# Splits, sums and casts beside the gate and up products in another order, and the norms' squares added on POOL behind each residual update

## The chip, the core and the metric

One core of a Trainium2 chip runs the whole program. The metric is the device time of one execution in microseconds (us). In the text PE is TensorE (its matrix product; PEld its weight load), DVE is VectorE, ACT is ScalarE, POOL is GpSimd, and SP is the engine whose queue issues most DMAs.

## The reference, cut to what matters

Two layers over 1024 latent tokens and 256 context tokens, width 1024, everything in float32. The last layer needs no context output.

```python
for l in range(DEPTH):                       # DEPTH = 2
    last = l == DEPTH - 1
    hl = modulate(rms_norm(x, norm1[l]), sh1, sc1)
    ...
    y_l, y_c = token_mixers(hl, hc, ...)     # attention, recurrence, gating unit, w_out
    x = x + g1[:, None] * y_l
    x = x + g2[:, None] * swiglu(modulate(rms_norm(x, norm2[l]), sh2, sc2), w_ffn_in[l], w_ffn_out[l])
    ...                                      # the same for the context, unless last
return rms_norm(x, final_norm)

def rms_norm(x, g):
    y = x * lax.rsqrt(jnp.mean(x * x, axis=-1, keepdims=True) + EPS)
    return y * g

def swiglu(h, w_in, w_out):
    g, u = jnp.split(h @ w_in, 2, axis=-1)   # w_in: 1024 x 2*2816
    return (jax.nn.silu(g) * u) @ w_out
```

## The kernel before, in words

**Precision.** A float32 operand of a product is split: a cast on ACT rounds it to `fp32r` (`wh`, `oh`), a subtraction on DVE keeps the rest (`wl`, `ol`), and three matmuls (high by high, high by rest, rest by high) make up one float32 product. The function `split` issues the cast and the subtraction.

**Gate and up.** The 2816 columns of gate and of up are 22 tiles `f` of 128 columns. For each tile the kernel computes `h @ gate` and `h @ up` for both halves of the 1024 tokens by a scheme of seven products in place of eight (P1 to P7). The left factors are blocks of the gate weights (A11, A12), of the up weights (A21, A22) and of their sums and differences (S1 to S4), the right factors are such combinations of the tokens. One product is 12 matmuls of 512 columns. In the first layer two more products per tile (CG and CU, 256 columns) serve the context. The products go to three PSUM banks `ffA`, `ffB`, `ffC` per tile, and `evacuate` takes the results out on ACT and DVE: copies `e`, sums, the gate's tanh, and the product of gate and up (`th<-th,e`).

**Sums of weights.** `prepare` splits the blocks. For tile `f` POOL computes, behind the split of A12, the four sums and differences S1 to S4 (`s<-wr`, `s<-wr,wr`, `wr<-wr,wr`, `wr<-wr,s`).

**Units.** `ffn_units` cuts the products into units of two whose weight blocks share one pair of tiles (`wh`, `wl`); there are two such pairs, so a unit's split waits until the unit two before it is through PE. In the last layer the seven products of a tile are three units of two and one unit of one (A22, P4). The splits of a unit are issued beside the products of the unit before it: the first block ahead of that unit's first product, the second ahead of its second one, and beside a unit of one both blocks ahead of its only product.

**Folding.** The results of two tiles (f even, f odd) are combined again, on POOL (`o<-th,th`, `th<-th,th`: four per two tiles), split (`oh` on ACT, `ol` on DVE) and written to DRAM (`pair<-oh`, `pair<-ol`) as the right factors of the seven products of the output projection. Generators do this, and `fold_step` moves each on by one step behind every product.

**Norms.** Behind each residual update `x<-op,mod,x` or `x<-fr,g2h,x` on DVE the squares of x are needed for the next norm. In the kernel before, a lane per piece of tokens does this: a lane is a generator that `fill` moves on where a model of the engines' clocks says that ACT and DVE have room. It squares on ACT (`sq<-x`) and adds on DVE (`acc<-acc,sq`). Then a matmul with ones (`ms<-acc,ones`) sums over the 1024 channels, ACT and DVE make the factor `r` of it, and DVE scales with it.

**Order.** Each engine takes its instructions in the order in which the program was written out. That order is fixed when the program is built, by the loops, the lanes and the clock model. In the first layer the gate and up stage also carries the vector work of the conditioning (`ada<-wr,cz,ada` on DVE, its matmuls `adt`), three steps per tile.

Every instruction is recorded with the line of the same helper (L117), so rows are told apart by their tiles.

Of the kernel before, what the change touches and what calls it, by code (L numbers as in the profile page):

```python
# [12 lines left out]
AF = mybir.ActivationFunctionType  # L13
# [109 lines left out]
def hybrid_block_kernel(  # L123
# [546 lines left out]
    written = {}  # L670

    def running_rinv(g, n, box):

        yield lambda: written.get(g, 0) > 0
        acc = temp(name="acc")[:, :n]
        for k in range(KT):
            yield lambda: written.get(g, 0) > k
            yield [x_at(k, g, n)]
            if k == 0:
                act(acc, x_at(k, g, n), AF.Square)  # L680
            else:
                sq = temp(name="sq")[:, :n]
                act(sq, x_at(k, g, n), AF.Square)
                tt(acc, acc, sq, op=OP.add)
        yield from rms_rinv([], n, D, box, acc)

    def running(pieces):

        boxes = {}
        for g, n in pieces:  # L690
            written.pop(g, None)
            boxes[g] = []
            Lane(running_rinv(g, n, boxes[g]), 4)
        return boxes
# [121 lines left out]
    for l in range(DEPTH):  # L816
# [916 lines left out]
        def out_proj(c):  # L1733
# [8 lines left out]
            for m in range(KT):  # L1742
# [12 lines left out]
                for g, n in OUTP[c]:  # L1755
# [11 lines left out]
                    written[g] = m + 1  # L1767
# [138 lines left out]
        def ffn_units():  # L1906
# [10 lines left out]
            if last:  # L1917
                units.append(([(f, "A22") for f in first], [(f, "P4") for f in first], (0, 1)))
            for f in range(NF):
                head = ([(f, "A11"), (f, "A12")], [(f, "P1"), (f, "P2")] + [(f, "CG")] * (not last), (0, 1))  # L1920
                body = [([(f, "S2"), (f, "S1")], [(f, "P6"), (f, "P5")], (0, 1))]
                body += [([(f, "S3"), (f, "S4")], [(f, "P7"), (f, "P3")], (0, 1))]
                if last:
                    tail = [([(f, "A22")], [(f, "P4")], (0, 0))]
                else:
                    tail = [([(f, "A22"), (f, "A21")], [(f, "P4"), (f, "CU")], (0, 1))]
                if f in first:
                    units += tail if not last else []
                elif f < NF - 1 or last:
# [7 lines left out]
        def ffn_in(side):  # L1937
# [7 lines left out]

            def prepare(u, i):
# [10 lines left out]
                if name == "A11":  # L1957
                    mine[f] = dict(zip("gu", (next_raw(False), next_raw(False))))
# [5 lines left out]
                if name == "A12":  # L1964
                    for s in ("s1", "s2"):
                        r[s] = temp(512, name=s).rearrange("p (k m) -> p k m", m=P)
                    if f < EARLY:
                        gp.tensor_tensor(r["s1"], u1, u2, op=OP.add)
                    gp.tensor_tensor(g1, g1, u1, op=OP.subtract)
                    gp.tensor_tensor(r["s2"], u2, g1, op=OP.subtract)  # L1970
                    if f >= EARLY:
                        gp.tensor_tensor(r["s1"], u1, u2, op=OP.add)
                    gp.tensor_tensor(g2, g2, r["s2"], op=OP.subtract)
# [52 lines left out]
            def fold_even(q, b11, b12):  # L2026
                h, t1 = r32("oh"), temp(name="o1")
                sc.copy(h, b11)
                gp.tensor_tensor(t1, b12, b11, op=OP.subtract)
                yield  # L2030
                lo, h1_ = r32("ol"), r32("oh")
                tt(lo, b11, h, op=OP.subtract)
                put(operand(q, "B11"), h, lo)
                sc.copy(h1_, t1)
                yield
                lo = r32("ol")
                tt(lo, t1, h1_, op=OP.subtract)
                put(operand(q, "T1"), h1_, lo)
                evens.add(q)

            def fold_odd(q, b22):
                while q not in evens:
# [544 lines left out]
```

## Time and profile before

| | us |
|---|---|
| median of 3 runs (lowest to highest) | 3146.05 (3144.38 to 3148.62) |
| the profiled execution's own time | 3144.73 |
| its span in the trace | 3142.4 |
| gate and up stage, first layer | 784.5 to 1417.8 |
| gate and up stage, last layer | 2363.5 to 2893.4 |
| output rest of the last layer, final norm | 3089.9 to the end |

The span runs from the first to the last instruction of the trace; the remaining 2.3 us of the execution's own time lie around it. Times in the text are positions in the span.

### The profile page before, as it was taken

To read this page: it belongs to the slowest core of one execution; us is meant where nothing else is said; L and a number is where in the kernel's file an instruction comes from. 1 tells how busy PE (TensorE), PEld (TensorE's weight loads), DVE (VectorE), ACT (ScalarE), POOL (GpSimd) and SP (SyncE) were. 2 spreads that over 40 slices of the span, in tenths; PEclk is the share of its full clock that TensorE was granted. 3 is DMA by queue.
4 is the path that set the end of the run, shared out by engine and by line. 5 is a ranking of instruction groups with operands and counts; after the bars stand their busy time and mean duration, and the time that the engine had idled before them with its cause. 6 is when DMAs were issued, how large, how long until landed. Compare 5 with 4: busy or idle time off the path is not lost. (4 is left out here: it accounts for less than half of the span.)

```text
span 3142.4 us, 38750 instructions
## 1 busy us (share of the span) xinstructions
PE 2884.7 (92%) x13774; PEld 2320.1 (74%) x13774; DVE 2169.4 (69%) x3306; ACT 1538.9 (49%) x2835; POOL 991.6 (32%) x802
## 2 busy tenths in 40 slices
PE   7999999999899999999998898999997888988996
PEld 4687677777678788887886687687685666666885
DVE  5675766765788877866667676666677555555887
ACT  5665688854533333332112676688755333333222
POOL 0001466600233333433221002467303454453330
PEclk8999999999899999999999899999998999999998
DMA  7302000043154454558462010000151433335861
GB/s 270 128 24 75 31 11 1 8 134 127 62 174 151 165 184 171 188 197 320 171 230 94 29 53 31 21 8 7 33 202 48 148 124 114 131 124 212 312 249 61
DMA packets 149394, 378.64 MB, mean 120 GB/s; under 512 B 15952, under 2 KB 28240, under 8 KB 149200
## 3 DMA queue, kind: packets, MB, share of 16 engines
q1 hardware_dynamic: 146576, 367.24, 32.9%
q0 software_dynamic: 2624, 8.91, 0.7%
q8 instruction: 109, 1.79, 0.2%
q14 instruction: 85, 0.70, 0.1%
HBM read 270.19 MB, written 105.91 MB: 120 GB/s over the span
## 5 line engine op out<-in xcount | busy, mean ns | idle before, releaser
L117 DVE TENSOR_TENSOR wl<-wr,wh 128x512 fp32r<-128x512 f32 (+2 forms) x433 | 344.3, 802 | 185.6 <-ACT wh L117 181.9
L117 ACT CAST wh<-wr 128x512 fp32r<-128x512 f32 (+2 forms) x433 | 274.1, 652 | 390.1 <-PE foX L117 201.2
L117 PE MATMUL ffA<-T,wh 128*128 128x512 f32 x1056 | 337.6, 400 | 17.6 <-DVE T L117 8.5
L117 POOL TENSOR_TENSOR pl<-pf,ph 128x512 fp32r<-128x512 f32 (+1 forms) x231 | 308.5, 1346 | 137.7 <-ACT ph L117 110.2
L117 PE MATMUL prj<-h,wh 128*128 128x384 f32 (+1 forms) x1056 | 260.3, 334 | 19.4 <-ACT h L117 11.7
L117 POOL TENSOR_TENSOR th<-th,e 128x512 f32<-128x512 f32 x44 | 64.5, 1465 | 617.6 <-DVE th L117 459.3
L117 ACT ACTIVATE pf<-s 128x512 f32<-128x512 f32 (+1 forms) x336 | 195.9, 589 | 115.1 <-PE s L117 110.4
L117 PEld LDWEIGHTS ffA<-T,wh 128*128 128x128 f32 x1056 | 197.7, 191 | 70.3 <-DVE T L117 11.1
L117 PEld LDWEIGHTS prj<-h,wh 128*128 128x128 f32 x1056 | 189.3, 198 | 42.6 <-ACT h L117 15.7
L117 PE MATMUL ffA<-T,wl 128*128 128x512 f32 x528 | 211.2, 400 | 10.3 <-DVE wl L117 10.1
L117 DVE TENSOR_TENSOR wl<-s,wh 128x512 fp32r<-128x512 f32 (+1 forms) x168 | 144.9, 864 | 108.6 <-ACT wh L117 107.3
L117 DVE TENSOR_REDUCE mx<-mx 128x1 f32<-128x512 f32 (+1 forms) x328 | 202.9, 680 | 20.2 <-PE mx L117 19.6
L117 ACT ACTIVATE th<-e 128x512 f32<-128x512 f32 x88 | 55.6, 632 | 309.6 <-DVE e L117 309.6
L117 PE MATMUL op<-y,wh 128*128 128x512 f32 (+1 forms) x576 | 181.7, 387 | 2.6 <-ACT y L117 2.0
L117 PE MATMUL prj<-h,wl 128*128 128x384 f32 (+1 forms) x528 | 170.6, 323 | 8.8 <-DVE wl L117 8.8
L117 POOL DMA_DIRECT2D ys<-y x20 | 11.1, 557 | 515.5 <-DVE y L117 514.8
L117 POOL TENSOR_TENSOR s<-wr 128x512 f32<-128x512 f32 (+1 forms) x84 | 91.5, 1089 | 257.7 <-DMA wr<-in_wfu_dram 256.8
L117 DVE SCALAR_TENSOR_TENSOR x<-foA,g2h,x 128x512 f32<-128x512 f32 x160 | 120.0, 750 | 59.2 <-PE foA L117 59.0
L117 PE MATMUL ffC<-T,wh 128*128 128x512 f32 x352 | 125.7, 438 | 35.1 <-ACT wh L117 21.7
L117 ACT CAST oh<-th 128x512 fp32r<-128x512 f32 x128 | 79.0, 617 | 160.7 <-POOL th L117 105.2
L117 PE MATMUL s<-qh,kh 97*128 97x512 f32 (+3 forms) x336 | 153.7, 458 | 4.0 <-ACT qh L117 1.8
L117 PE MATMUL foA<-T,wh 128*128 128x512 f32 x480 | 149.6, 393 | 5.8 <-DVE x L117 5.8
(342 smaller groups left out, 8047.3 us busy)
## 6 DMA issues: line engine op xcount, KB each, us to landing
wr<-in_wada_dram SPq DMA_DIRECT2D x80, 512.0 KB, 3.9
pair<-oh SPq DMA_DIRECT2D x140, 256.0 KB, 2.3
pair<-ol SPq DMA_DIRECT2D x140, 256.0 KB, 2.0
T<-pair SPq DMA_DIRECT2D x60, 512.0 KB, 9.8
wr<-in_wfg_dram SPq DMA_DIRECT2D x44, 512.0 KB, 3.8
wr<-in_wfu_dram SPq DMA_DIRECT2D x44, 512.0 KB, 4.7
wr<-in_wfo_dram SPq DMA_DIRECT2D x80, 256.0 KB, 4.7
B<-pair SPq DMA_DIRECT2D x40, 512.0 KB, 7.9
```

The costliest lines, as they stand in the source:

```text
L117: return f(*args, **kw)
```

## The change

- `ffn_units`, last layer: the seven products of each tile from the third on are laid end to end over all tiles and cut by twos. There is no unit of one any more, and a unit can hold P4 of one tile and P1 of the next.
- `open_tile`: the two sums S1 and S2 of the next tile are issued on POOL behind P7 (last layer) or P3 (first layer) of the tile before, and no longer behind the split of A12. S2 is computed from S1.
- Folding: one step later (`yield` first), one cast to a step, and in the last layer the four combinations per two tiles go to DVE (`add_up`). A new temporary `o4` takes one of them.
- The product of gate and up goes to DVE always; `either`, which chose POOL or DVE by the clock model, is gone.
- Norms: `Running` squares on ACT directly behind each residual update, and adds on POOL the square of the update before. The lanes are gone.
- `room`, which limits the lanes that are open at a time, is 12 instead of 14 beside the output projection of the mixers.

In numbers over the whole program: 70 additions of squares go from DVE to POOL; 44 products of gate and up and 40 combinations go from POOL to DVE. No matmul, cast or DMA is added or removed.

```diff
-    def running_rinv(g, n, box):
-        yield lambda: written.get(g, 0) > 0
-        acc = temp(name="acc")[:, :n]
-        for k in range(KT):
-            yield lambda: written.get(g, 0) > k
...
-                act(sq, x_at(k, g, n), AF.Square)
-                tt(acc, acc, sq, op=OP.add)
-        yield from rms_rinv([], n, D, box, acc)
+    class Running:
+        def add(self, k):
+            sq = temp(name="sq")[:, : self.n]
+            act(sq, x_at(k, self.g, self.n), AF.Square)
+            self.flush()
+            if self.acc is None:
+                self.acc = sq
+            else:
+                self.late = sq
+            if k == KT - 1:
+                self.flush()
+                Lane(rms_rinv([], self.n, D, self.box, self.acc), 2, True)
+        def flush(self):
+            if self.late is not None:
+                gp.tensor_tensor(self.acc, self.acc, self.late, op=OP.add)
+                self.late = None
...
-                    written[g] = m + 1
+                    norms[g].add(m)
...
+            if last:
+                seq = [(f, *bp) for f in range(EARLY, NF) for bp in zip(
+                    ("A11", "A12", "S2", "S1", "S3", "S4", "A22"), ("P1", "P2", "P6", "P5", "P7", "P3", "P4")
+                )]
+                for i in range(0, len(seq), 2):
+                    two = seq[i : i + 2]
+                    units.append(([t[:2] for t in two], [t[::2] for t in two], (0, 1)))
+                return units
...
-                if last:
-                    tail = [([(f, "A22")], [(f, "P4")], (0, 0))]
...
+            def open_tile(f):
+                r = mine[f] = dict(zip("gu", (next_raw(False), next_raw(False))))
+                for s in ("s1", "s2"):
+                    r[s] = temp(512, name=s).rearrange("p (k m) -> p k m", m=P)
+                gp.tensor_tensor(r["s1"], r["u"][:, 0:4, :], r["u"][:, 4:8, :], op=OP.add)
+                gp.tensor_tensor(r["s2"], r["s1"], r["g"][:, 0:4, :], op=OP.subtract)
...
                 if name == "A12":
...
                     gp.tensor_tensor(g1, g1, u1, op=OP.subtract)
-                    gp.tensor_tensor(r["s2"], u2, g1, op=OP.subtract)
-                    if f >= EARLY:
-                        gp.tensor_tensor(r["s1"], u1, u2, op=OP.add)
                     gp.tensor_tensor(g2, g2, r["s2"], op=OP.subtract)
...
+            add_up = tt if last else gp.tensor_tensor
+            def fold(q, name, src):
+                h = r32("oh")
+                sc.copy(h, src)
+                yield
+                lo = r32("ol")
+                tt(lo, src, h, op=OP.subtract)
+                put(operand(q, name), h, lo)
...
             def fold_odd(q, b22):
+                yield
                 while q not in evens:
                     yield
                 b11, b12 = inputs.pop((2 * q, 1)), inputs.pop((2 * q, 0))
-                h = r32("oh")
-                sc.copy(h, b22)
-                gp.tensor_tensor(b12, b22, b12, op=OP.subtract)
-                yield
...
+                add_up(b12, b22, b12, op=OP.subtract)
+                yield from fold(q, "B22", b22)
+                add_up(b11, b12, b11, op=OP.add)
...
-                    either(a, a, u, OP.mult)
+                    tt(a, a, u, op=OP.mult)
...
+                    if p == ("P7" if last else "P3") and EARLY <= f < NF - 1:
+                        open_tile(f + 1)
```

**ACT, last layer, around P3 and P4 of tile 13 and P1 of tile 14.** `e` are copies out of PSUM, `th` the gate's tanh, `oh` the fold's casts, `wh` the casts of weight blocks; `wr_23274` (before) and `wr_23270` (after) are the gate weights of tile 14. Before:

```order
L117 COPY e_23418<-ffC_23405 128x512
L117 CAST wh_23420<-wr_23107 128x512
L117 ACTIVATE th_23454<-e_23401 128x512
L117 CAST oh_23458<-th_23454 128x512
L117 CAST wh_23461<-wr_23274 128x512 x2
L117 CAST oh_23491<-th_23304 128x512
L117 CAST wh_23493<-s_4651_23468 128x512
```

After:

```order
L117 COPY e_23420<-ffC_23407 128x512
L117 CAST wh_23403<-wr_23112 128x512
L117 CAST wh_23449<-wr_23270 128x512
L117 ACTIVATE th_23466<-e_23399 128x512
L117 CAST wh_23449<-wr_23270 128x512
L117 CAST oh_23488<-th_23466 128x512
L117 CAST wh_23490<-s_4651_23446 128x512
```

The first cast of tile 14 stands ahead of the tanh now, its second one behind the tanh but ahead of the fold's cast `oh`.

**POOL, the same place.** `s` and `wr` are sums of weights, `o` and `th<-th,th` combinations of the fold, `th<-th,e` the product of gate and up. Before:

```order
L117 TENSOR_TENSOR th_23454<-th_23454,e_23418 128x512
L117 TENSOR_TENSOR th_23304<-th_23454,th_23304 128x512
L117 TENSOR_TENSOR wr_23274<-wr_23274,wr_23276 128x512
L117 TENSOR_TENSOR s_4651_23468<-wr_23276,wr_23274 128x512
L117 TENSOR_TENSOR s_4650_23467<-wr_23276 128x512
L117 TENSOR_TENSOR wr_23274<-wr_23274,s_4651_23468 128x512
L117 TENSOR_TENSOR th_23215<-th_23304,th_23215 128x512
```

After:

```order
L117 TENSOR_TENSOR wr_23110<-wr_23110,wr_23112 128x512
L117 TENSOR_TENSOR wr_23110<-wr_23110,s_4627_23294 128x512
L117 TENSOR_TENSOR s_4650_23445<-wr_23272 128x512
L117 TENSOR_TENSOR s_4651_23446<-s_4650_23445,wr_23270 128x512
L117 TENSOR_TENSOR wr_23270<-wr_23270,wr_23272 128x512
L117 TENSOR_TENSOR wr_23270<-wr_23270,s_4651_23446 128x512
```

Only the four sums of weights are left on POOL in this stage, and the two for S1 and S2 stand ahead of the two that write into `wr`.

**ACT, first layer to last layer, beside the first projections of the last layer.** `h<-ht,mod` are normed operands, `xr` copies of projections, `acc` and `sq` squares. Before:

```order
L117 ACTIVATE h_15542<-ht_15543,mod_105 128x128
L117 ACTIVATE acc_15548<-x_12774 128x512
L117 ACTIVATE sq_15550<-x_12774 128x512
L117 CAST wh_15553<-wr_15088 128x1024
L117 COPY xr_15442<-prj_15559 128x384
L117 ACTIVATE sq_15585<-x_12864 128x512
L117 ACTIVATE sq_15588<-x_12864 128x512
L117 COPY xr_15442<-prj_15591 128x256
```

After:

```order
L117 ACTIVATE h_15585<-ht_15586,mod_105 128x128
L117 ACTIVATE h_15524<-ht_15591,mod_105 128x512
L117 CAST wh_15594<-wr_15098 128x1024
L117 COPY xr_15485<-prj_15600 128x384
L117 ACTIVATE h_15529<-ht_15626,mod_105 128x512
L117 COPY xr_15485<-prj_15630 128x256
```

The squares of tokens 0 to 511 stood here; they have gone ahead of these projections, behind the updates, and the normed operands of 512 columns stand in their place.

## Rows read from the trace of the kernel before

**Rows 1.** The page's busy times over the whole span.

```profile
PE 2884.7 (92%) x13774; PEld 2320.1 (74%) x13774; DVE 2169.4 (69%) x3306; ACT 1538.9 (49%) x2835; POOL 991.6 (32%) x802
```

**Rows 2.** Busy time by stretch: length, then each engine, granted clock, DMA share, GB/s.

```profile
core 0: us, PE busy (x) PEld busy (x) DVE busy (x) ACT busy (x) POOL busy (x), PEclk, DMA share, GB/s
2444.60:2893.40 448.80, 398.24 (x1598) 298.42 (x1597) 254.71 (x315) 161.95 (x294) 202.29 (x134) 0.98 0.37 133
2703.10:2749.70 46.60, 42.49 (x170) 31.84 (x168) 26.83 (x33) 17.03 (x31) 21.39 (x15) 0.96 0.34 124
2707.20:2709.80 2.60, 2.60 (x7) 2.00 (x6) 1.23 (x2) 0.20 (x1) 2.52 (x3) 0.50 0.20 72
2872.00:2891.20 19.20, 19.19 (x83) 15.61 (x84) 11.76 (x15) 6.71 (x12) 6.37 (x5) 1.00 0.68 253
2425.20:2444.60 19.40, 19.37 (x86) 15.53 (x84) 13.93 (x18) 9.01 (x18) 10.83 (x8) 1.00 0.48 159
860.40:1417.80 557.40, 529.41 (x2754) 447.13 (x2752) 434.74 (x598) 207.80 (x383) 211.38 (x139) 0.98 0.52 177
887.00:1164.80 277.80, 260.72 (x1344) 220.13 (x1343) 224.50 (x312) 105.32 (x192) 106.58 (x70) 0.97 0.47 159
1164.80:1270.60 105.80, 103.89 (x554) 88.34 (x554) 81.41 (x110) 40.00 (x74) 43.07 (x28) 1.00 0.52 180
```

**Rows 3.** PE's timeline, last layer: start, length, instruction, idle before and releaser.

```profile
2425.21 0.61 PE L117 MATMUL ffA<-B,wh 128*128 128x512 f32 x2
...
2703.10 0.39 PE L117 MATMUL ffA<-T,wl 128*128 128x512 f32 x1
2705.46 0.73 PE L117 MATMUL ffA<-B,wh 128*128 128x512 f32 x2 [1.98 <-ACT wh L117]
...
2712.95 0.62 PE L117 MATMUL ffA<-T,wh 128*128 128x512 f32 x2
...
2715.66 0.61 PE L117 MATMUL ffC<-T,wh 128*128 128x512 f32 x2
...
2893.37 0.74 PE L117 MATMUL foA<-B,wh 128*128 128x512 f32 x2 [1.76 <-ACT wh L117]
```

**Rows 4.** ACT's timeline in the same place.

```profile
2704.27 0.62 ACT L117 CAST oh<-th 128x512 fp32r<-128x512 f32 x1 [2.11 <-POOL th L117]
2704.80 1.14 ACT L117 CAST wh<-wr 128x512 fp32r<-128x512 f32 x2
```

**Rows 5.** POOL's timeline in the same place.

```profile
2704.32 1.27 POOL L117 TENSOR_TENSOR th<-th,th 128x512 f32<-128x512 f32 x1
2706.22 1.67 POOL L117 TENSOR_TENSOR wr<-wr,wr 128x512 f32<-128x512 f32 x1 [0.63 <-DVE wl L117]
...
2710.77 1.75 POOL L117 TENSOR_TENSOR wr<-wr,s 128x512 f32<-128x512 f32 x1
```

**Rows 6.** DVE's timeline in the same place.

```profile
2706.66 0.68 DVE L117 TENSOR_TENSOR th<-th,ffA 128x512 f32<-128x512 f32 x1
...
2711.28 1.78 DVE L117 TENSOR_TENSOR ol<-th,oh 128x512 fp32r<-128x512 f32 x1
...
2718.68 0.68 DVE L117 TENSOR_TENSOR wl<-wr,wh 128x512 fp32r<-128x512 f32 x1
```

**Rows 7.** Who waited for whom, PE, 860.4 to 1417.8: total, times, longest.

```profile
PE ffA L117 <- DVE wl L117: 9.2, 6, 2.5
PE adt L117 <- DVE ada L117: 7.0, 4, 3.0
PE ffA L117 <- DVE e L117: 6.7, 7, 2.3
```

**Rows 8.** PE's timeline, first projections of the last layer.

```profile
1745.77 0.28 PE L117 MATMUL prj<-h,wl 128*128 128x256 f32 x1
1750.15 2.07 PE L117 MATMUL ms<-acc,ones 128*128 128x512 f32 x2 [4.11 <-DVE acc L117]
...
1757.84 1.48 PE L117 MATMUL prj<-h,wh 128*128 128x384 f32 x2 [5.62 <-ACT h L117]
```

**Rows 9.** DVE's and PE's timelines at the end of the program.

```profile
3115.23 5.38 DVE L117 SCALAR_TENSOR_TENSOR x<-x,cols,r 128x512 f32<-128x512 f32 x8
3126.40 2.07 PE L117 MATMUL ms<-acc,ones 128*128 128x512 f32 x2 [11.88 <-DVE acc L117]
3130.56 0.69 DVE L117 SCALAR_TENSOR_TENSOR v<-ms,v 128x512 f32<-128x512 f32 x1 [4.21 <-ACT v L117]
3132.47 5.39 DVE L117 SCALAR_TENSOR_TENSOR x<-x,cols,r 128x512 f32<-128x512 f32 x8
```

More of the change, by code (lines that the diff above doesn't have):

```diff
@@ L1731, in hybrid_block_kernel, with out_proj @@
             fill()
-        def out_proj(c):
+        def out_proj(c, norms):
             w, pss = {}, {}
@@ L2067, in fold_odd, with fold_rest @@
                 b21 = inputs.pop((2 * q + 1, 1))
-                h = r32("oh")
-                sc.copy(h, b21)
-                gp.tensor_tensor(b11, b21, b11, op=OP.subtract)
-                yield
-                lo = r32("ol")
-                tt(lo, b21, h, op=OP.subtract)
-                put(operand(q, "B21"), h, lo)
-                h = r32("oh")
-                sc.copy(h, b11)
-                yield
-                lo = r32("ol")
-                tt(lo, b11, h, op=OP.subtract)
-                put(operand(q, "T4"), h, lo)
-            def fold_rest(f, c, a):
+                t4 = temp(name="o4")
+                add_up(t4, b21, b11, op=OP.subtract)
+                yield from fold(q, "T2", b11)
+                yield from fold(q, "B21", b21)
+                yield from fold(q, "T4", t4)
+            def fold_rest(f, c, a):
+                yield
                 h = r32("oh")
@@ L2175, in ffn_in @@
                 fold_step()
-        def either(out, a, b, op):
-            n = math.prod(out.shape[1:])
-            if line.clock["pool"] + n / 400 < line.clock["dve"] + n / 960 + 0.07:
-                gp.tensor_tensor(out, a, b, op=op)
-            else:
-                tt(out, a, b, op=op)
         CONTEXT_AT = (("B21", "T4"), ("T3", "B22"))
@@ L2345, in hybrid_block_kernel, with ffn_rest @@
         wrest = []
-        def ffn_rest(c):
+        def ffn_rest(c, norms):
             rest = group[-1]
@@ L2410, in hybrid_block_kernel @@
         Lane(finish_chunk(0, OUTP[0]), 4)
-        boxes1 = running(OUTP[1])
-        pace(out_proj(1))
+        norms, boxes1 = running(OUTP[1])
+        room[0] = 12
+        pace(out_proj(1, norms))
         ensure(lambda: len(complete_ys[0]) == KT)
@@ L2434, in hybrid_block_kernel @@
         pace(ffn_out())
-        last_boxes = running(RESTP[1])
-        pace(ffn_rest(1))
+        norms, last_boxes = running(RESTP[1])
+        pace(ffn_rest(1, norms))
         if last:
@@ L2454, in hybrid_block_kernel @@
             Lane(modulated(h1[0], [part_of(HT, CH - HT, HT, ())], am1, mods[1], 0), 6)
-        last_boxes.update(running(RESTP[0]))
-        pace(ffn_rest(0))
+        norms, boxes = running(RESTP[0])
+        last_boxes.update(boxes)
+        pace(ffn_rest(0, norms))
         wrest.clear()
```

73 lines of the change are left out of this document (22 added, 51 removed).

## The prediction

> **What bounds the kernel now.** I read the page's busy times first: PE 92%, DVE 69%, ACT 49%, POOL 32% of the span [rows 1]. PE is the bound, so I look for stretches in which it idles or runs slowly, and for who is late there. The windows by stage [rows 2] single out gate and up of the last layer. PE's timeline there [rows 3] gives the floor: a product begins at 2712.95 and the next at 2715.66, 2.71 us for twelve matmuls, 19.0 us for a tile of seven. Tile 2 begins at 2425.21 and the output projection at 2893.37, so tiles 2 to 21 take 468.16 us, 23.41 each, 4.4 above the floor and 87 us over 20 tiles (20 x 7 x 2.72 = 380.8). At the start of the same stage, before any folding, tile 2 took 19.40 us, and the last tile, with five POOL instructions, 19.20 [rows 2].
>
> Between two tiles the loss is in the open. P4 ends near 2703.5 (2703.10 + 0.39), P1 starts at 2705.46 after 1.98 us on ACT's `wh` [rows 3]. ACT issued that cast at 2704.80, behind a fold cast `oh` that had waited 2.11 us for POOL's `th` [rows 4]; POOL began another combination at 2704.32, 1.27 us long [rows 5]. The fold, which nothing needs soon, holds up the weights, which PE needs now. The loss goes on: in 2707.2 to 2709.8 the granted clock was 0.50, 1.2 instead of 2.4 GHz, right behind PE's gap [rows 2].
>
> **Last layer, gate and up.** Per two tiles DVE has 33 instructions and POOL 14 of its own (the window shows 15, one of them cut by its edge) in 46.6 us [rows 2]; afterwards they are 39 and 8. (1) The four combinations go to DVE, where `oh` no longer waits for POOL, and the next tile's two casts stand ahead of `oh`. (2) No unit of one is left, so the second block of a unit is always split behind the unit's first product. Take the case shown in the order, the split of A12 issued behind P3: ahead of it DVE has `e`, a gate product, a product, some 3.0 us with ACT's tanh between, then `wl` 0.68, so 3.7 us; it is wanted two products later, 2 x 2.72 + 0.45 = 5.9 us. Some 2.2 us are left. (3) S1 and S2 are asked of POOL a product earlier, and four POOL instructions remain per tile against eight in tile 2's window.
>
> The nearest row is tile 2: DVE x18 and 13.93 us, POOL x8 and 10.83 us, 19.40 us for the tile with PE busy 19.37 [rows 2]. Afterwards DVE has 19.5 per tile, one and a half more at 0.68 each [rows 6], or 1.0 us: 15 of 19.4. I take 19.40: 20 x 19.40 = 388, so **-80**. The bounds: -87 at the floor; and, at the other end, each of a tile's four POOL sums falls on one DVE instruction that is wanted. Beside POOL's 1.75 us sum [rows 5] DVE's `ol` took 1.78 in place of 0.68 [rows 6]; four times 1.1 is 4.4 us, less the slack of 2.2, so 2.2 us lost per tile, 44 in all, and a gain of **-36**.
>
> DVE's `th<-th,ffA`, one operand in PSUM, took 0.68 (from 2706.66) inside POOL's 1.67 us sum from 2706.22, and a two-SBUF subtraction away from POOL also 0.68 [rows 5, 6]. The Trainium skill (SBUF — State Buffer, section "Who interferes with whom") says that a DVE instruction with two SBUF inputs and a GpSimd one that reads SBUF take turns on a shared port, one wholly blocking the other. The trace agrees as far as it goes: 1.78 is about 0.68 plus a large part of one POOL instruction. By that rule moving work between these two engines frees nothing while both still run; what frees is that fewer POOL instructions are there to collide with. Rival B is this rule taken to its end.
>
> **Hand-over to the output projection.** PE waits 1.76 us there [rows 3]. The last folds lose their POOL steps but begin a step later; I take **-2**, bounds -2 and 0.
>
> **First layer, gate and up.** PE is busy 529.41 of 557.40 us, so 28.0 are idle; the first ten tiles take 27.8 us each, the four after 26.45 [rows 2]. Its longest waits are on DVE: `wl` 9.2, `ada` 7.0, `e` 6.7 [rows 7]. DVE is busy 224.5 of 277.8 us (81%) while the conditioning runs beside it, 77% behind it [rows 2]. The change adds to DVE at most one product per tile that POOL used to take, 0.68 us [rows 6]: at worst, if all fall on the path, +14 over 20 tiles. It takes from the path POOL's four sums in one burst behind A12 (now two and two), and the casts behind POOL's combinations (now a step later). The best case is all 28 us and the clock's 0.02 of 529 us, -38. Between these I take half of the idle time, **-15**.
>
> **Between the layers.** The first projections of the last layer wait for the norm: PE stops 4.11 us for `acc`, runs `ms`, then 5.62 us for `h` [rows 8]. With the squares behind the updates all `ms` are done before these projections, and `h` comes from the scaling alone. Of 9.7 us I take **-8**; bounds -11 (with 1.4 of the `ms` matmul's 2.07 if it moves into a gap) and +3, if the scaling of the second half is now what is late.
>
> **End of the program.** Before, DVE puts eight scalings of the first half (5.38 us from 3115.23) ahead of the second half's sums, so `ms` waits until 3126.40, 11.88 us [rows 9]. Now the last update is followed by a square on ACT (0.62, as a cast of that size [rows 4]) and one POOL addition, 1.27 [rows 5]: `ms` at about 3117.5. From `ms` to the scalings it is 6.1 us (3126.40 to 3132.47): 3123.6. But both halves' scalings are now at the end: 5.4, then the second half's step from `v` (1.9, 3130.56 to 3132.47), then 5.4: 3136.3 against 3137.86 [rows 9], **-1.6**.
>
> **The other norms.** 70 additions leave DVE (0.68) for POOL (1.27) [rows 5, 6]: off DVE in the output stages, but only the last one is on a path, there 0.6 us longer at each `ms`. The Trainium skill (GPSIMD Engine Reference, section 3) calls GpSimd the wrong engine for ordinary elementwise work, about twice as slow as VectorE (1.96x); the rows have 1.9x. By that rule alone each of some six norm ends would lose 0.6 us, about 4 us more than I put down. I take **0**, bounds -4 (DVE freed of a few additions ahead of an update) and +4. What hides the additions is that an update comes only every few us; without that cover 70 x 0.6 would be 42 us.
>
> Sum: -80 - 2 - 15 - 8 - 1.6 + 0 = -106.6. From the profiled execution's 3144.73 that is 3038.1; the median of the runs lies 1.3 above that execution, so **3040**.
>
> **Rivals.**
> A is the forecast: 3040, its own range 3015 to 3062 (all terms near their good bounds, or last layer at 20.3 per tile and no gain in the first).
> B: POOL's sums and DVE's subtractions collide on the path and the last layer gains only 36: 44 more than A, 3084. For it: DVE's 1.78 us instructions [rows 6]. Against: tile 2 had twice the POOL instructions and lost nothing [rows 2].
> C: the first layer is bound by DVE while the conditioning runs, and the extra products cost 14 in place of a gain of 15: 3069. For it: 81% busy and the waits on `wl` and `ada` [rows 2, 7]. Against: the four tiles behind the conditioning lose little.
> D, the other side: DVE becomes the bound of the last layer. Of the 39 instructions per two tiles, 31 take both operands from SBUF. With n of them at 1.78 and the rest at 0.68 two tiles take 26.5 + 1.1 n; that passes 46.6 at n = 19, and outweighs the 27 us gained elsewhere from n = 21. At n = 25 it is 54.0, +74 over ten pairs, and the whole 3145 + 74 - 27 + 1 = 3193. Against: eight POOL instructions per pair can stretch eight or nine, which gives 36 us, under the 38.8 that PE needs.
> E: the change doesn't do what it says, since the heads of the tiles wait on something else (a weight buffer, a landing DMA): the last layer stays and the rest gives 27, 3120. Against: the releaser named at the head is ACT's cast, and the chain behind it leads to POOL [rows 3 to 5].
>
> **How the numbers follow.** About 0.2% (6 us) is what a measurement of this kernel can tell from no change. Chances: A 0.60, B 0.20, C 0.12, D 0.05, E 0.03. Faster: A, B, C and E less a little, 0.93; same 0.02; slower 0.05. The range: 3012, where A's terms lie near their better bounds (the whole of them would be near 3000), to 3088, which takes in B and C and leaves out D, E and B together with C: 3012 to 3088.
>
> **What would show it.** Last layer: pitch of a tile near 19.4, granted clock 1.0 throughout, no waits of PE's P1 on ACT's `wh`, POOL x8 and DVE x39 per two tiles; B would show DVE instructions of 1.78 us just ahead of PE's waits on `wl`, D a DVE busy above 95%. First layer: the first ten tiles nearer 26.5 than 27.8; C would show more waits on `wl` and `e` than 9.2 and 6.7. Between the layers no `ms` behind the first `prj`. At the end `ms` near 3117 (shifted by what was gained) and sixteen scalings in a row but for the short step. Wrong I would be if the POOL additions of squares hold up `ms` by several us at every norm, or if the folds, a step later, leave the output projection waiting.

## The result, and the profile after

The changed kernel takes 3030.69 us (median of 4 runs, 3027.88 to 3032.64) against 3146.83 us for the kernel before in the same comparison: a ratio of 0.9631, 95% interval 0.9614 to 0.9647. The forecast was 3040. The profiled execution took 3032.14 us, its span is 3030.3.

The page's busy times first (as [rows 1]):

```profile
PE 2839.1 (94%) x13774; PEld 2319.5 (77%) x13774; DVE 2179.0 (72%) x3320; ACT 1536.5 (51%) x2835; POOL 937.3 (31%) x788
```

PE has the same 13774 instructions; they are busy 45.6 us less. The rest of the 112 us of span is idle time that is gone. The clock is only a part of the 45.6. In tiles 2 to 21 of the last layer the granted clock was 0.98 before (PE busy 417.6 of 468.2 us, from 2425.2 to 2893.4), and 2% of 468 us are some 9 us; now it is 1.00, and PE is busy 36.8 us less there. What the clock leaves is put down to waits too short to show: a matmul's row lasts 0.39 us, but 140 x 12 of them take 380.8 us after the change, 0.23 each, so a wait of up to 0.16 us behind one counts as busy.

Where the time went shows in the windows of the changed kernel (columns as in [rows 2]): last layer, tiles 2 to 21; two tiles of it; first layer, tiles 2 to 21, and its two parts; the mixers' output projection of the last layer.

```profile
2403.33:2784.13 380.80, 380.80 (x1682) 315.31 (x1680) 301.62 (x392) 171.23 (x312) 114.11 (x84) 1.00 0.46 161
2590.00:2628.10 38.10, 38.10 (x170) 31.55 (x169) 30.35 (x39) 17.04 (x31) 11.34 (x9) 1.00 0.43 152
865.86:1396.05 530.19, 519.08 (x2754) 446.25 (x2753) 440.87 (x618) 205.88 (x385) 180.61 (x119) 0.99 0.53 186
865.90:1089.50 223.60, 212.49 (x1099) 179.94 (x1098) 203.25 (x285) 85.83 (x159) 72.53 (x48) 0.97 0.52 174
1089.50:1396.00 306.50, 306.50 (x1658) 266.26 (x1657) 237.57 (x334) 120.04 (x226) 108.03 (x72) 1.00 0.55 194
2239.15:2339.90 100.75, 93.22 (x391) 71.66 (x389) 62.81 (x80) 49.77 (x72) 16.96 (x14) 1.00 0.48 167
```

In the last layer PE is busy in all of the 380.80 us: 140 products of 2.72 us, the floor itself, with the granted clock at 1.00. The two windows of the first layer part it: up to 1089.5 PE idles 11.1 us, from there on none. The last line is a loss: the projection took 93.6 us before (2269.9 to 2363.5), 100.7 now.

ACT's timeline at a tile's end in the last layer, and PE's at the first product of this tile and of the next (compare [rows 3, 4]; P1 of the next tile starts at 2612.77):

```profile
2605.35 0.62 ACT L117 CAST oh<-th 128x512 fp32r<-128x512 f32 x1
2605.86 0.62 ACT L117 CAST wh<-wr 128x512 fp32r<-128x512 f32 x1
2606.39 0.62 ACT L117 CAST oh<-o 128x512 fp32r<-128x512 f32 x1
2606.91 0.62 ACT L117 CAST wh<-wr 128x512 fp32r<-128x512 f32 x1
2611.02 0.63 ACT L117 ACTIVATE th<-e 128x512 f32<-128x512 f32 x1 [3.49 <-issue]
```

```profile
2593.73 0.62 PE L117 MATMUL ffA<-B,wh 128*128 128x512 f32 x2
...
2612.77 0.62 PE L117 MATMUL ffA<-B,wh 128*128 128x512 f32 x2
```

The fold's casts still stand between the weight casts, but in these rows no cast has an idle time in brackets (only the tanh has), and PE's first product has none either: 19.04 us from tile to tile. In all of tiles 2 to 21 the fold's casts wait 9.7 us, for DVE and at most 1.0 us at a time, and PE loses nothing by it.

The stages one by one, in us, from the first PE instruction of one to that of the next (head: tiles 0 and 1; body: tiles 2 to 21, with the hand-over to the output projection). These lengths are worked out from PE's timelines of the two kernels:

| stage | before | after | change | forecast |
|---|---|---|---|---|
| mixers' output projection, first layer | 130.4 | 133.6 | +3.2 | 0 |
| gate and up, first layer, head | 75.9 | 79.2 | +3.3 | - |
| gate and up, first layer, body | 557.4 | 530.2 | -27.2 | -15 |
| output rest to the next layer's `sv` | 132.1 | 123.6 | -8.5 | -8 |
| mixers' output projection, last layer | 93.6 | 100.8 | +7.2 | 0 |
| gate and up, last layer, head | 61.7 | 63.4 | +1.7 | - |
| gate and up, last layer, body | 468.2 | 380.8 | -87.4 | -82 |
| output rest and end | 52.5 | 49.8 | -2.7 | -1.6 |
| all else | 1570.6 | 1568.9 | -1.7 | - |
| span | 3142.4 | 3030.3 | -112.1 | -106.6 |

### The profile page after: what moved, and what is told of

It is laid out like the page before. It is cut to its first block, busy times and chain, and to the rows that moved or that the text cites. A ratio compares the mean times of both kernels' runs of the same rounds, so it can differ in the third digit from the quotient of the medians.

```text
span 3030.3 us, 38783 instructions
## 1 busy us (share of the span) xinstructions
PE 2839.1 (94%) x13774; PEld 2319.5 (77%) x13774; DVE 2179.0 (72%) x3320; ACT 1536.5 (51%) x2835; POOL 937.3 (31%) x788
## 4 chain that ended last, share of the span: by engine, by line
PE 63%; DVE 12%; ACT 5%; DMA 3%; issue 2%; POOL 1%; DVEq 0%; SPq 0%; ACTq 0%; POOLq 0%
PE ffA L117 14%; PE foA L117 7%; PE ffC L117 6%; PE pv L117 5%; PE s L117 5%; PE op L117 3%; PE ffB L117 3%; PE foC L117 3%; PE prj L117 3%; PE ffCU L117 2%; DVE wl L117 2%; PE ffCG L117 2%; PE foX L117 2%; PE foB L117 2%; DVE x L117 2%
## 5 line engine op out<-in xcount | busy, mean ns | idle before, releaser
L117 DVE TENSOR_TENSOR wl<-wr,wh 128x512 fp32r<-128x512 f32 (+2 forms) x433 | 364.8, 844 | 164.5 <-ACT wh L117 162.1
L117 PE MATMUL prj<-h,wh 128*128 128x384 f32 (+1 forms) x1056 | 259.6, 333 | 17.6 <-ACT h L117 7.9
L117 ACT ACTIVATE pf<-s 128x512 f32<-128x512 f32 (+1 forms) x336 | 195.7, 588 | 114.1 <-PE s L117 109.5
L117 POOL TENSOR_TENSOR sq<-sq,sq 128x512 f32<-128x512 f32 (+1 forms) x70 | 82.8, 1187 | 307.6 <-ACT sq L117 305.5
L117 DVE TENSOR_TENSOR wl<-s,wh 128x512 fp32r<-128x512 f32 (+1 forms) x168 | 156.6, 935 | 16.8 <-ACT wh L117 16.7
L117 POOL DMA_DIRECT2D ys<-y x20 | 11.1, 553 | 498.9 <-DVE y L117 498.1
L117 ACT ACTIVATE ph<-s 128x512 fp32r<-128x512 f32 x242 | 141.5, 585 | 1.2 <-POOL qf L117 1.0
L117 PEld LDWEIGHTS op<-y,wh 128*128 128x128 f32 x576 | 109.3, 191 | 29.6 <-ACT wh L117 3.0
```

The source lines that it names most:

```text
L117: return f(*args, **kw)
```

## The experiments

Two theories on the last layer. ORDER, the forecast's: weight casts stood on ACT behind fold casts that wait, with too little time between split and use. LOAD, rival B at its end: POOL's combinations and products themselves are the loss. Then two on the norms, SQUARE and POOL ADD. The times are medians; "body" is that of the table.

**Only the pairs.** The kernel before with this edit:

```
+            if last:
...
+                for i in range(0, len(seq), 2):
+                    two = seq[i : i + 2]
+                    units.append(([t[:2] for t in two], [t[::2] for t in two], (0, 1)))
+                return units
...
```

> The kernel before, with only the units of the last layer cut by twos over all tiles; folds, sums, products on POOL and norms as before. Theory ORDER (the 87 us of the last layer were lost because weight casts stand on ACT behind fold casts that wait, with too little time left before PE wants the block; time between split and use is what counts): a block then is always split two products before its use, so more than half comes back although POOL keeps its 14 instructions per two tiles: tiles 2 to 21 of the last layer 385 to 425 us (before 468.2, after 380.8), whole 3065 to 3105. Theory LOAD (POOL's combinations and products themselves are the loss: they stretch DVE and hold ACT): tiles 2 to 21 stay above 445 us, whole 3122 to 3147.

Measured: 3125.00 us, ratio 0.9942 (0.9927 to 0.9956); body of the last layer 453.3. The wait at the tile's head is gone, the one in the middle is not. ACT's, POOL's and PE's timelines there:

```profile
2698.43 0.62 ACT L117 CAST oh<-th 128x512 fp32r<-128x512 f32 x1 [3.50 <-POOL th L117]
2698.96 0.61 ACT L117 CAST wh<-s 128x512 fp32r<-128x512 f32 x1
```

```profile
2690.35 1.74 POOL L117 TENSOR_TENSOR wr<-wr,wr 128x512 f32<-128x512 f32 x1
2692.17 1.63 POOL L117 TENSOR_TENSOR s<-wr,wr 128x512 f32<-128x512 f32 x1
2693.76 1.26 POOL L117 TENSOR_TENSOR s<-wr 128x512 f32<-128x512 f32 x1
2694.98 1.73 POOL L117 TENSOR_TENSOR wr<-wr,s 128x512 f32<-128x512 f32 x1
2696.68 1.73 POOL L117 TENSOR_TENSOR th<-th,th 128x512 f32<-128x512 f32 x1
```

```profile
2699.62 0.73 PE L117 MATMUL ffC<-T,wh 128*128 128x512 f32 x2 [1.44 <-ACT wh L117]
```

Read backwards: PE waits for the cast of S1, which stands behind a fold cast, which waits 3.50 us for POOL's combination, which stands behind four sums. A pair's two products of lead are not enough for that queue. ORDER's number (385 to 425) fell; LOAD's held here.

**No pairs.** The changed kernel with the old units of the last layer:

```
-                    units.append(([t[:2] for t in two], [t[::2] for t in two], (0, 1)))
...
+                if last:
+                    tail = [([(f, "A22")], [(f, "P4")], (0, 0))]
```

> The changed kernel, with the last layer's units cut as before (three of two and one of one per tile). ORDER: both blocks of the next tile's first unit are split beside P4 alone and wanted 2.7 us later, behind two casts of 1.14 us and two subtractions of 0.68 us on engines that also have the tanh and the gate products of P3: 1 to 3 us lost per tile, tiles 2 to 21 at 400 to 440 us, whole 3050 to 3090. LOAD: POOL has 8 instructions per two tiles, so tiles 2 to 21 stay within 8 us of 380.8, whole 3031 to 3039.

Measured: 3050.22 us, ratio 0.9703 (0.9689 to 0.9718); body 399.2. PE's waits in it:

```profile
PE ffA L117 <- DVE wl L117: 12.1, 19, 1.0
```

One wait per tile, 0.6 us each, now on DVE's half of the split. ORDER's ranges hold but for 0.8 us of the body, LOAD's fall. So 18.4 of the 87.4 us hang on the pairs once all else is done, and 14.9 when nothing else is (453.3 against 468.2).

**Combinations on POOL again.**

```
-            add_up = tt if last else gp.tensor_tensor
+            add_up = gp.tensor_tensor
```

> The changed kernel, with the four combinations per two tiles on POOL again in the last layer, so 12 POOL and 35 DVE instructions per two tiles. ORDER: a fold's cast may wait on ACT for POOL, about 2 us each time, in front of a weight cast; the 2.2 to 5 us between split and use cover most of it: tiles 2 to 21 at 381 to 395 us, whole 3031 to 3045. LOAD: each of four combinations costs about the 1.1 us by which a neighbour on DVE is stretched or more, 40 us or more over ten pairs: tiles 2 to 21 above 415 us, whole above 3065.

Measured: 3032.79 us, ratio 0.9649 (0.9634 to 0.9663); body 381.4, with POOL busy 176.7 us in it in place of 114.1. ORDER's ranges hold. LOAD falls: 40 instructions more on POOL cost 0.6 us.

**Sums late.**

```
                 if name == "A12":
...
                     gp.tensor_tensor(g1, g1, u1, op=OP.subtract)
+                    gp.tensor_tensor(r["s2"], u2, g1, op=OP.subtract)
+                    if f >= EARLY:
+                        gp.tensor_tensor(r["s1"], u1, u2, op=OP.add)
                     gp.tensor_tensor(g2, g2, r["s2"], op=OP.subtract)
...
-                    if p == ("P7" if last else "P3") and EARLY <= f < NF - 1:
-                        open_tile(f + 1)
```

> The changed kernel, with the four sums of weights behind the split of A12 again, in both layers, as in the kernel before. ORDER: the cast of S2 stands on ACT until POOL is through two sums more (1.3 to 1.7 us each, four in one burst): 1 to 3 us lost per tile in the last layer, tiles 2 to 21 at 395 to 430 us; in the first layer it takes part of the 27 us back, tiles 2 to 21 there at 535 to 550 us (before 557.4, after 530.1). LOAD: same number of POOL instructions, so last layer within 8 us of 380.8. Whole by ORDER 3050 to 3100, by LOAD 3031 to 3045.

Measured: 3040.75 us, ratio 0.9676 (0.9660 to 0.9692); bodies 533.3 (first layer) and 381.3. In the last layer next to nothing, in the first 3.1 us. That is no more than this stage varies by: in runs whose edits leave it alone it took 525.2 (**Combinations on POOL again**) to 530.6 us (**Square one update later**). ORDER as I had put it falls too: no single cast that waits explains the loss. (6.5 us of the rest are in the attention stage, which the edit doesn't touch; see the last section.)

**Folds early.** The generators as before, `add_up` as changed:

```
             def fold_even(q, b11, b12):
-                t1 = temp(name="o1")
-                yield
+                h, t1 = r32("oh"), temp(name="o1")
+                sc.copy(h, b11)
                 add_up(t1, b12, b11, op=OP.subtract)
...
```

> The changed kernel, with the generators of the folds as before (no first step of waiting, up to two casts to a step), combinations still on DVE in the last layer. Theory FOLDS: the fold's step later is what freed the casts in both layers; then tiles 2 to 21 of the first layer go back by 10 us or more (530.1 to above 540) and those of the last layer lose 1 us or more per tile (above 400). Theory SLACK: pairs and earlier sums leave enough time, so the step costs under 8 us in either layer, whole 3031 to 3045.

Measured: 3052.05 us, ratio 0.9702 (0.9684 to 0.9721); bodies 547.8 and 385.5. In the first layer FOLDS holds: the generators' new form, a step later and one cast to a step, is worth 17.6 of its 27.2 us. In the last it is worth 4.7, as SLACK has it.

**Folds early and on POOL.** The last edit, and with it

```
-            add_up = tt if last else gp.tensor_tensor
+            add_up = gp.tensor_tensor
```

> The changed kernel, with two edits undone together: the folds' generators as before and their combinations on POOL. Each alone cost the last layer's tiles 2 to 21 almost nothing (385.5 and 381.4 us against 380.8). Theory CHAIN (what was lost needs all of: a fold cast that is issued at once, so that it waits on ACT for POOL, a POOL that is late because the combination stands behind the sums of weights in one burst, and a weight cast behind it on ACT): with the sums still early and split in two bursts POOL is at hand, the cast waits one combination (1.3 to 1.7 us), within the slack: 385 to 400 us, whole 3042 to 3065. Theory PAIR OF TWO (a fold cast that waits for POOL is enough): 415 to 455 us, whole above 3070.

Measured: 3071.86 us, ratio 0.9770 (0.9755 to 0.9786); body 402.5. The body lies between the two theories and nearer to CHAIN; the whole lies where PAIR OF TWO has it, because the folds' generators cost the first layer 17.1 us again (547.3). PE's waits in the body, the longest three, then ACT's timeline ahead of one of the third kind (PE's `ffC` goes on at 2511.00):

```profile
PE ffA L117 <- DVE e L117: 3.9, 9, 0.4
PE ffA L117 <- ACT e L117: 1.9, 9, 0.2
PE ffC L117 <- ACT e L117: 1.6, 9, 0.2
```

```profile
2509.32 0.62 ACT L117 CAST oh<-th 128x512 fp32r<-128x512 f32 x1 [1.59 <-POOL th L117]
2509.85 0.61 ACT L117 CAST wh<-wr 128x512 fp32r<-128x512 f32 x1
2510.37 0.58 ACT L117 COPY e<-ffC 128x512 f32<-128x512 f32 x1
```

So the chain ends elsewhere than CHAIN has it. PE waits for no weight cast here, but for the copies and sums `e` that empty its PSUM banks, and the copy stands on ACT behind the same fold cast that waits for POOL. These waits come to 8.7 us in all with those on `wl`; the rest of the 21.7 us lost is put down to gaps too short to be listed.

**And the sums late.** The last two edits, and with them

```
-                gp.tensor_tensor(r["s1"], r["u"][:, 0:4, :], r["u"][:, 4:8, :], op=OP.add)
...
                 if name == "A12":
...
+                        gp.tensor_tensor(r["s1"], u1, u2, op=OP.add)
...
```

> As the run with early folds on POOL, and the four sums of weights behind the split of A12 again; so of the last layer's stage only the pairs of units and the product of gate and up on DVE are left of the change. CHAIN: now the combination stands behind the burst of sums and the fold cast behind it, in front of the cast of S1: 430 to 455 us, near the 453.3 of the kernel before with pairs alone, and 30 us or more above the run with early folds on POOL. PAIR OF TWO: within 10 us of that run. A third way: below 400, then the product on POOL was needed too.

Measured: 3096.73 us, ratio 0.9848 (0.9833 to 0.9863); body 424.0. Who waited in the bodies, ACT without and with late sums, then PE with them (total, times, longest; PE without them stands above):

```profile
ACT oh L117 <- POOL th L117: 46.1, 27, 3.3
...
ACT wh L117 <- PE ffA L117: 14.3, 10, 1.8
```

```profile
ACT oh L117 <- POOL th L117: 48.9, 27, 3.5
ACT wh L117 <- POOL s L117: 27.7, 10, 2.8
```

```profile
PE ffC L117 <- ACT wh L117: 13.0, 9, 1.4
PE ffA L117 <- ACT e L117: 8.2, 17, 0.7
```

Only with late sums does POOL hold a weight cast on ACT (27.7 us), and only then is PE back at the wait on `wh` in `ffC`. That gives a ladder of the last layer's body: 380.8, with early folds 385.5, with those on POOL 402.5, with late sums 424.0, with the product on POOL too 453.3 (the pairs alone), with units of one 468.2. Steps that cost 4.7, 0.6 and 0.5 us alone cost 43.2 together. CHAIN is right in direction, its sizes are off (402.5 where at most 400, 424.0 where at least 430 was expected), and its last link, the weight cast, is shown only with late sums. The last step but one, 29.3 us, is put down to the product by elimination: the runs differ in that, in the norms, which leave this body at 380.8 (next run), and in `temp` buffers; it was not run alone. With the pairs alone PE waits in `ffC` for `wh` 18 times, 26.0 us, in place of 9 times.

**Norms by lanes.** The old `running_rinv` in place of `Running`, `room` 14:

```
-                    norms[g].add(m)
+                    written[g] = m + 1
...
-        room[0] = 12
```

> The changed kernel, with the norms by lanes as before (squares where the clock model has room, additions on DVE, room 14 throughout): the whole worth of the norm part. The two profiles say: output projection of the mixers 93.6 us before and 100.7 after in the last layer, 784.5 and 786.7 at the start of gate and up in the first; transition 8.3 and end 2.7 us shorter after. If these are all due to the norms, undoing gains 7 and 2 and loses 8 and 3: whole within 5 us of 3030.7. A rival, that the scheduling of everything else shifted them: then the projection of the last layer stays near 100.

Measured: 3026.93 us, ratio 0.9623 (0.9605 to 0.9641), so not to be told from the changed kernel. The stages part it: projections back at 130.5 and 93.6, transition back at 132.4, output rest and end at 52.1. The new norms gain 11.1 us in two stages and lose 10.3 in two others. The heads are shorter here too, 76.5 and 61.1.

**Additions on DVE.**

```
-                gp.tensor_tensor(self.acc, self.acc, self.late, op=OP.add)
+                tt(self.acc, self.acc, self.late, op=OP.add)
```

> The changed kernel, with the squares' additions on DVE, at the same places. Theory SQUARE (the 7 us that the last layer's output projection of the mixers lost come from ACT's square directly behind each update, which waits for DVE with the next weight cast behind it): projection still 98 to 102 us; only the last addition before each sum over channels is 0.6 us shorter or longer, whole 3025 to 3036. Theory POOL ADD (they come from POOL's additions, which hold DVE or come late): projection back at 93 to 96 us, whole 3020 to 3026.

Measured: 3015.81 us, ratio 0.9589 (0.9576 to 0.9602); projection of the last layer 97.3, between the two theories; the whole is below both. So POOL's additions have a part in the 7 us, and the square has one. The heads are 6.0 and 1.8 us shorter, the first layer's body 5.1, the last no more than that stage varies by (525.2 to 530.6, above).

**Square one update later.**

```
         def add(self, k):
+            if k > 0:
+                self.square(k - 1)
             if k == KT - 1:
+                self.square(k)
...
```

> The changed kernel, with the square of each update issued one update later (the last two together), additions still on POOL. SQUARE: the square finds its x ready, ACT no longer stands in front of the weight cast: last layer's output projection of the mixers 93 to 96 us in place of 100.7, about 1 us lost at each of the norms' ends, whole 3022 to 3028. POOL ADD: projection stays at 98 to 102 us, whole 3029 to 3036.

Measured: 3010.00 us, ratio 0.9572 (0.9559 to 0.9585); projections 128.1 and 93.8. First ACT, DVE and PE in the changed kernel, then ACT with the later square:

```profile
2281.00 0.63 ACT L117 ACTIVATE sq<-x 128x512 f32<-128x512 f32 x1 [0.64 <-DVE x L117]
2281.54 1.04 ACT L117 CAST wh<-wr 128x1024 fp32r<-128x1024 f32 x1
```

```profile
2280.23 0.74 DVE L117 SCALAR_TENSOR_TENSOR x<-op,mod,x 128x512 f32<-128x512 f32 x1
2282.61 1.54 DVE L117 TENSOR_TENSOR wl<-wr,wh 128x1024 fp32r<-128x1024 f32 x1 [1.64 <-ACT wh L117]
```

```profile
2284.21 0.50 PE L117 MATMUL op<-y,wl 128*128 128x512 f32 x1 [0.78 <-DVE wl L117]
```

```profile
2266.14 0.63 ACT L117 ACTIVATE sq<-x 128x512 f32<-128x512 f32 x1
2266.67 1.04 ACT L117 CAST wh<-wr 128x1024 fp32r<-128x1024 f32 x1
```

Before: update, square that waits for it, weight cast, subtraction, and PE 0.78 us late. With the later square this square finds its x ready, and the cast behind it doesn't wait. Only the last square, at 2272.35, still waits 4.06 us for the update, and PE loses nothing there. SQUARE holds; all 7 us are back. The whole fell further than SQUARE has it: of the 23.1 us between the two profiles 12.5 are in the projections, and 4.4 in the attention stage, which the edit doesn't touch.

**Conditioning mixed, square later.** The last edit, and column groups that need two sums now alternate with those that need one:

```
-    BESIDE = [(0, 40), (0, 44)] + [(1, b) for b in range(0, 48, 4)]
+    BESIDE = [(0, 40), (1, 16), (0, 44), (1, 20)]
+    for b in range(0, 16, 4):
+        BESIDE += [(1, b), (1, 24 + b)]
+    BESIDE += [(1, 40), (1, 44)]
```

> The changed kernel, with each square issued one update later, and with the conditioning's column groups that need two sums alternating with those that need one, in place of the six heavy ones first. The tiles 2 to 9 of the first layer (27.9 us each, DVE 91% busy) lose to the heavy groups; the later ones, with light groups, lose nothing (25.5 us, DVE 78%). If DVE's load there is the cause, an even load of about 86% leaves 515 to 522 us for tiles 2 to 21 of the first layer in place of 530.2 (and 530.6 with the square later alone), whole 2994 to 3005. If the loss has another cause (a landing of the conditioning's weights, the steps of the context product), it stays at 527 to 532, whole 3006 to 3014.

Measured: 3005.68 us, ratio 0.9562 (0.9548 to 0.9575); first layer's body 521.7, as DVE's load would have it, and below every run with the old order (525.1 at the least). The rival, a landing, has no row: in tiles 2 to 9 of the changed kernel DVE never waits for a landing of the conditioning's weights; behind them it does, 5.2 us in all, and PE idles none. The whole is just above the expected 3005, and its interval overlaps that of the later square alone: the stage is 8.9 us shorter, but the attention stage was 4.6 longer in this profile.

**And additions on DVE.** The run before with

```
-                gp.tensor_tensor(self.acc, self.acc, self.late, op=OP.add)
+                tt(self.acc, self.acc, self.late, op=OP.add)
```

> As the run with the mixed conditioning and the later squares, with the squares' additions on DVE. Additions on DVE alone gained 15 us on the changed kernel and later squares alone 21. If both come from the same wait (ACT's square in front of the weight cast), they don't add: within 4 us of the run without it. If the addition on POOL costs of itself (0.6 us longer in front of each sum over channels, and a held-up DVE), another 6 to 12 us are gained: 2985 to 2997.

Measured: 3013.31 us, ratio 0.9585 (0.9572 to 0.9598): 7.6 us more, not less, by the medians; the two intervals just touch. The first layer's projection is 133.4 in place of 128.1, where PE's `ms` waits 7.0 us in all on DVE's `sq` (1.9 on POOL's without this edit). The last layer's is 93.7 in both. Both theories fall: with the square out of the way the addition on POOL is the better place.

So the fastest are the two with the later square, on POOL: 3010.0 and 3005.7 us, 0.6 to 0.7% below the changed kernel by their ratios.

## Why the prediction was right, point by point

**Last layer.** Right in place and sign, and mis-sized by 5 us: I took tile 2's 19.40 us per tile; it came to 19.04, PE's floor, with the hand-over's 1.76 us gone as well. The miss is 7 us, in truth: the 468.16 us end at 2893.37, behind that wait, so the hand-over's -2 was counted a second time. DVE's load was put at 15 of 19.4 us per tile; it measured 30.35 per two, of 38.1. The working gave three causes as if each brought a part. The runs show chains from POOL over ACT's fold casts, of which each of combinations on DVE, earlier sums and later folds breaks enough: undone singly they cost 0.6, 0.5 and 4.7 us. Only the pairs matter singly, 18.4.

**Rival B** (a gain of 36 us only) fell with the combinations on POOL at 381.4 us. Collisions there are: in the changed kernel POOL's sum and DVE's subtraction overlap in these rows.

```profile
2604.19 1.54 POOL L117 TENSOR_TENSOR s<-s,wr 128x512 f32<-128x512 f32 x1 [1.37 <-ACT wh L117]
```

```profile
2604.49 1.78 DVE L117 TENSOR_TENSOR wl<-wr,wh 128x512 fp32r<-128x512 f32 x1
```

DVE's 0.68 became 1.78 and POOL's 1.29 became 1.54, and PE felt nothing. The two take 2.08 us from the start of the one to the end of the other, about the sum of their lengths alone. The rule on the shared port (the Trainium skill, SBUF — State Buffer, "Who interferes with whom"), by which two such instructions contend, agrees with these rows; that one waits wholly for the other does not show, since POOL began first and got longer too. What it costs depends on the lead of the split, and here it was covered. The prediction's subtraction "away from POOL" [rows 6] was in truth beside POOL: a combination began at 2718.91, 0.23 us after it, and took 1.61 us, and the subtraction kept its 0.68. **D** fell with DVE at 79% of the last layer's stretch, **E** with the wait at the head gone in every run with pairs.

**First layer.** The sign was right, the term mis-sized: -27.2 for -15. Half of the 28 idle us was a choice between bounds; what is left is 11.1 us, all in tiles 2 to 9. There, too, one sentence of the working was wrong: the conditioning does not end at 1164.8. Its groups that need two sums (`adt<-sel`) start for the last time at 1109.2, and the light ones (`adt<-ones`) go on to 1404.8, all in the kernel before. The mixed order shows that the heavy groups cost: 521.7 us. Of the 27.2, the folds' generators and the earlier sums bring 20.3 together: with both undone (**And the sums late**) the stage takes 550.5. The remaining 6.9 are left to the product on DVE by elimination, since the norms by lanes leave the stage at 529.2; it was not run alone. **C** fell: of the waits of `ffA` and `adt` on DVE, that on `wl` shrank from 9.2 us [rows 7] to 0.2 and that on `ada` from 7.0 to 1.2; only that on `e` grew, from 6.7 to 9.1. The changed kernel's waits, 862 to 1396 (total, times, longest):

```profile
PE ffA L117 <- DVE e L117: 9.1, 6, 2.9
PE adt L117 <- DVE ada L117: 1.2, 2, 1.0
...
PE ffA L117 <- DVE wl L117: 0.2, 1, 0.2
```

**Between the layers.** -8.5 for -8, by working that was wrong, so that the number fits is luck. I saw one stop of PE, of 9.7 us, and said that it goes. There were two before; one remains, as long as the first was:

```profile
1716.10 1.22 PE L117 MATMUL ms<-acc,ones 128*128 128x256 f32 x2 [6.96 <-DVE acc L117]
1721.20 1.34 PE L117 MATMUL prj<-h,wh 128*128 128x384 f32 x2 [3.88 <-ACT h L117]
```

```profile
1691.10 3.78 PE L117 MATMUL ms<-sq,ones 128*128 128x512 f32 x4 [5.06 <-POOL sq L117]
1700.58 1.34 PE L117 MATMUL prj<-h,wh 128*128 128x384 f32 x2 [5.71 <-ACT h L117]
```

The first fence is the kernel before, its first stop, 10.8 us; the second the changed kernel, 10.8 us. The second stop of before, [rows 8], has no counterpart but 2.1 us on `h`.

**End.** -2.7 for -1.6; both `ms` stand behind the last product, the second waited 2.11 us for POOL, and the pair of matmuls took 1.13 us in place of 2.07 (last section).

**The other norms: the step that failed.** I put 0, bounds -4 and +4, and priced the additions, 0.6 us each at the ends. The two projections lost 10.4 us. The price was in the main not in what moved to POOL but in what stayed on ACT and moved up: a square directly behind an update waits for DVE, and the next weight cast waits behind the square. Shown by the later square (-7.0 and -5.5 us in the projections). In the first layer's projection the same chain ends at `ms`. There a sign of being wrong that the prediction had named came true: `ms` waited 4.39 and 1.95 us for POOL's additions, where it had waited 2.33 and 1.49 for DVE's. ACT's, DVE's, POOL's and PE's timelines of the changed kernel at the longer of these:

```profile
699.93 0.63 ACT L117 ACTIVATE sq<-x 128x512 f32<-128x512 f32 x1 [0.71 <-DVE x L117]
700.47 1.04 ACT L117 CAST wh<-wr 128x1024 fp32r<-128x1024 f32 x1
```

```profile
701.54 1.53 DVE L117 TENSOR_TENSOR wl<-wr,wh 128x1024 fp32r<-128x1024 f32 x1 [1.98 <-ACT wh L117]
702.99 0.74 DVE L117 SCALAR_TENSOR_TENSOR x<-op,mod,x 128x512 f32<-128x512 f32 x1
```

```profile
704.54 1.31 POOL L117 TENSOR_TENSOR sq<-sq,sq 128x512 f32<-128x512 f32 x1 [2.55 <-ACT sq L117]
```

```profile
705.90 1.65 PE L117 MATMUL ms<-sq,ones 128*128 128x512 f32 x2 [4.39 <-POOL sq L117]
```

The cast stands behind the square, the subtraction and the last update behind the cast, and the last square, its addition and `ms` behind that update. With the later square the first of the two waits is gone, the second (1.89) stays. POOL's additions do have a part: moved to DVE with the squares left in place they gave back half of the last layer's 7 us.

POOL's addition is nearly twice as long as DVE's, 1.29 against 0.68 us. The Trainium skill (GPSIMD Engine Reference, section 3) says about twice for such work, and these rows agree. It decides nothing: with the later square, POOL was the faster place by 7.6 us. The heads' +5.0 us I didn't forecast; they were 72.8 to 79.2 and 61.0 to 67.4 in the runs, and why isn't settled. A part may be spread: the kernel before and the one with pairs alone are the same up to there, and their first heads took 75.9 and 72.8.

The two errors in size (+5.4 and +12.2 us of gain missed) outweighed the loss that I missed (15.4 with the heads). That the sum came closer than its terms is luck.

## What to carry to other kernels

Ask of every instruction that may wait what stands behind it on its own engine: a cast that nobody needs soon, or a square that follows its update at once, costs what the urgent instruction behind it is late. A stall fed by a chain over several engines can go when one link is cut, so gains of single edits neither add up nor can be read from undoing them one by one; build up from the other side too. When work is moved to another engine, price what stays behind and moves up as well.

## What the runs showed of the hardware that was not expected

The same pair of `ms` matmuls took 2.07 us before and 1.13 us after. Before, PE had idled 11.88 us ahead of it [rows 9] and the granted clock was 0.50 (1.2 GHz); after, PE had idled 2.11 us and the clock was still 1.00 (2.4 GHz). With the later square PE idled 6.07 us ahead of the pair, the clock was 0.50 and the pair took 2.08. The windows, before, after and with the later square:

```profile
3126.40:3128.40 2.00, 2.00 (x2) 0.50 (x2) 0.00 (x0) 0.00 (x0) 0.00 (x0) 0.50 0.00 0
```

```profile
3004.20:3008.30 4.10, 1.99 (x5) 0.44 (x3) 0.75 (x1) 3.25 (x5) 2.84 (x3) 1.00 0.00 0
```

```profile
2989.70:2991.80 2.10, 2.06 (x2) 0.50 (x2) 2.10 (x4) 0.00 (x0) 0.00 (x0) 0.50 0.13 51
```

And the attention stage, whose work none of these edits touches, took 455.3 us in one profile (granted clock 0.97) and 467.6 in another (0.95). Differences of some 10 us between whole kernels are therefore read by stage here, not from the medians alone.
